# A two-block hybrid transformer on one core: first norm's weight row spread by TensorE, token sums in two steps, head halves joined by engines

## The chip, the cores and the metric

The kernel runs on one core of one Trainium2 chip. The metric is the device time of one execution in microseconds; the median of three runs stands for a kernel. One execution is also recorded by the hardware profiler, and all rows below are from that one. PE is TensorE's matmul side and PEld its weight loads, DVE is VectorE, ACT is ScalarE, POOL is GpSimd, SP is the engine that issues the DMAs.

## The reference, cut to what matters

All is float32: 512 tokens, 16 meta tokens ahead of them, width 1024.

```
def _rmsnorm(x, g): return x * rsqrt(mean(x*x) + EPS) * g

first block (once):
  h    = _rmsnorm([meta, x], norm_pre)                 # one weight row of 1024
  fox  = 8 causal heads of 64, decay bias; times silu(gate)
  mla  = 8 chunk-masked heads of 64 from low-rank q, kv; times silu(gate)
  x    = x + _rmsnorm([fox, mla] @ w_out, norm_post)

second block (two layers):
  h    = rms_norm(x, norm1)
  y_a .. y_d = mlstm, gqa (8 heads of 64), neighbourhood (8 heads of 64), differential attention
  x    = x + (sum_b sigmoid(gl_b) * (y_b @ w_up_b)) @ w_out
  h2   = rms_norm(x, norm2)
  x    = x + (silu(h2 @ w_gate) * (h2 @ w_up)) @ w_down     # d_ff = 2816 = 22 tiles of 128
out = rms_norm(x, final_g)
```

## The kernel before, in words

**Products.** A float32 operand is held as two float32r parts, `hi` and `lo`, and each product is three matmuls, hi·hi, lo·hi and hi·lo (`mm3`, L250 to L252). A weight tile is loaded as `raw`, rounded to `whi` by ACT (L221), and the rest `wlo` is taken by POOL or, every second or each time, by DVE (L223, `k.lo`). Results of PE stand in one of eight PSUM banks (`A`).

**Order.** PE runs in the order in which the program is written. For the other engines and the DMA issues a planner makes the order of each queue ahead of time, from estimated costs and from when the slots of the tile rings come free; on the chip each queue then runs strictly in its order. A tile tag is a ring of so many slots: `t2` six, `yn` three, `qs` two, `cb` two, `p` four.

**The start** (`first_block`, L681). SP loads token tile 0 in two halves, then the weight row `norm_pre`, spread by DMA over 128 partitions in two halves (`gain_row`, L528: tile `cb`), then token tiles 1 to 3 and the meta tokens. Each token tile is squared and summed by ACT (L720), scaled by DVE (L540), transposed by PE in eight pieces (L316) and split into `hi` and `lo` (L211, L212). The first weight product (`proj_late`, L268, matmuls L280) runs in two halves of 256 tokens; before the first half stand the transposes of tiles 0, 1 and 2, before the second that of tile 3 (`late_steps`, L152).

**Heads of 64** (`class Head`, L408; fox, mla, and branches b and c of both layers). The value tile of a head holds hi and lo side by side, so a head's output bank has two halves, partitions 0 to 63 and 64 to 127, that have to be added. After the last value matmul (L455) ACT copies the whole bank into a `t2` tile `z` (L458). When both heads of a pair are done, `pair_out` (L460) sends the upper half of one and the lower half of the other to the other partitions by two DMAs (L464, L465), and two DVE adds (L466, L467) make the joined tile `e`, which is gated or split. There are 24 pairs.

**The feed-forward** (`ffn`). Its 22 tiles of `d_ff` go in 11 pairs. The first pair runs as plain products: two gate tiles (each followed by `silu2`, L365 and L366, into `t2`), then two up tiles. Later pairs run as `fast_pair` (L582), a Strassen-Winograd scheme with seven products instead of eight; it needs sums of quarters of the tokens' activations, made once per layer by `Tokens.sums` (L563): two halves, each four DVE sums (L571 to L574) and for four results one ACT rounding (L576) and one DVE rest (L577). The quarters stand in two `qs` and two `cst` tiles. Those two `qs` slots also take the weights of the second member of each fast pair (`other` in `w_cols`), so the first such load waits until the sums have read a `qs` tile. In `fast_pair` the sums of weight blocks are L599 to L602, their rounding L591, the rest L592.

Of the kernel before, what the change touches and what calls it, by code (L numbers as in the profile page):

```python
# [18 lines left out]
P = 128  # L19
# [146 lines left out]
def hybrid_kernel(ctx: ExitStack, tc: tile.TileContext, i: dict, out: bass.AP):  # L166
# [241 lines left out]
    class Head:  # L408

        def __init__(self, v, blocks, meta=None):
            self.v, self.blocks, self.meta, self.pt, self.pm = v, blocks, meta, {}, {}

        def trans(self, t, p, col):

# [20 lines left out]
        def pv(self, t):  # L438

            if t % 2 == 0:  # L440
                return
            if t == 1:
                self.ps = bank()
            first, second = self.blocks(t - 1), self.blocks(t)
            ph, pl = self.pt[t // 2]
            parts = [(self.meta[0], *self.pm[t // 2], 0, 256)] if self.meta else []
            for b in sorted(set(first) | set(second), key=lambda b: not (b in first and b in second)):
                lo, hi = (0 if b in first else P), (256 if b in second else P)
                parts.append((self.v(b), ph[:, b], pl[:, b], lo, hi))
            o = (t // 2) * 256  # L450
            for j, (v, ph, pl, lo, hi) in enumerate(parts):
                last = j == len(parts) - 1
                passes = [(v, ph, P), (v[:, 0:64], pl, 64)]
                for w, q, m in (passes[::-1] if last else passes):
                    T_.matmul(self.ps[0:m, o + lo:o + hi], w, q[:, lo:hi], start=(j == 0 and m == P), stop=(last and m == P))  # L455
            if t == 3:
                self.z = t2()
                A_.copy(self.z, self.ps)  # L458

    def pair_out(heads):  # L460

        a, b = (h.z for h in heads)
        e = t2()
        nc.sync.dma_start(e[0:64], a[64:128])  # L464
        nc.sync.dma_start(e[64:128], b[0:64])  # L465
        V.tensor_tensor(e[0:64], a[0:64], e[0:64], ALU.add)  # L466
        V.tensor_tensor(e[64:128], b[64:128], e[64:128], ALU.add)  # L467
        return e

    def split_y(y, hi, lo):  # L470
        A_.copy(hi, y)
# [85 lines left out]
    class Tokens:  # L557
# [5 lines left out]
        def sums(self):  # L563

            (b11, b12), (b21, b22) = self.q
            hi = new(pool, [P, 4, 4, 256], "v", F32R, 1)
            lo = [new(pool, [P, 2, 4, 256], "ks", F32R) for _ in range(2)]
            self.t = [(hi[:, j], lo[j // 2][:, j % 2]) for j in range(4)]
            for c in (slice(0, 2), slice(2, 4)):
                t = [t2().rearrange("p (k c) -> p k c", k=2) for _ in range(4)]  # L570
                V.tensor_tensor(t[0], b12[:, c], b11[:, c], ALU.subtract)  # L571
                V.tensor_tensor(t[1], b22[:, c], t[0], ALU.subtract)
                V.tensor_tensor(t[2], b22[:, c], b12[:, c], ALU.subtract)
                V.tensor_tensor(t[3], b21[:, c], t[1], ALU.subtract)  # L574
                for j in (1, 2, 0, 3):
                    A_.copy(self.t[j][0][:, c], t[j])  # L576
                    V.tensor_tensor(self.t[j][1][:, c], t[j], f(self.t[j][0][:, c]), ALU.subtract)  # L577

        def quarter(self, a, b):
            return tuple(z[:, 4 * a:4 * a + 4, 256 * b:256 * b + 256] for z in self.h)  # L580
# [100 lines left out]
def first_block(k):  # L681
    nc, i, new, pool, A_, V, bank = k.nc, k.i, k.new, k.pool, k.A_, k.V, k.bank
    with k.tc.tile_pool(name="fb", bufs=1) as fb:
        k.fb = fb
        x, xm = new(pool, [P, NT, D], "x", bufs=1), new(pool, [NMETA, D], "v", bufs=1)
        for half in range(2):
            nc.sync.dma_start(x[:, 0, half * 512:half * 512 + 512], i["x"][0:P, half * 512:half * 512 + 512])
        gain = k.gain_row(i["norm_pre"], "cb")
        for t in range(1, NT):
            nc.sync.dma_start(x[:, t], i["x"][t * P:(t + 1) * P])  # L690
        nc.sync.dma_start(xm, i["meta"])
        cols = k.load(fb, i["cols_first"], "colsf")

        def col(name, n=P):
            a, w = COLS_FIRST[name]
            return cols[0:n, a:a + w]

        ss, hl = new(k.small, [P, 8], "xss"), k.act()
        h = k.tokens(hl)
        sm, xms = new(k.small, [P, 1], "mss")[0:NMETA], new(pool, [NMETA, D], "ks")  # L700

        def meta():
            A_.activation(xms, xm, AF.Square, accum_out=sm)
            r = k.rstd(sm, D, 1, NMETA)
            for half in range(2):
                sl = slice(half * 512, half * 512 + 512)
                V.scalar_tensor_tensor(xms[:, sl], xm[:, sl], r, gain[half][0:NMETA], ALU.mult, ALU.mult)

            def second():
                ps = bank()[:, 0:KD * NMETA]  # L710
                for kk in range(KD):
                    k.transpose(ps[:, kk * NMETA:(kk + 1) * NMETA], xms[:, kk * P:(kk + 1) * P], NMETA)
                k.evict_split(ps.rearrange("p (k c) -> p k c", k=KD), *(a[:, :, 0:NMETA] for a in hl))

            return second

        pending = []
        for t in range(NT):
            for half in range(2):
                A_.activation(k.t2(), x[:, t, half * 512:half * 512 + 512], AF.Square, accum_out=ss[:, 2 * t + half:2 * t + half + 1])  # L720
            pending.append(k.norm_tile(x[:, t], t, ss, h, gain))
        pending.append(meta())
        k.late = late_steps(pending[:-1]) + pending[-1:]
        k.constants()
        return first_body(k, fb, col, hl)


def first_body(k, fb, col, hl):
# [276 lines left out]
    def fox_head(hd):  # L1005
        u, e = fox.units[hd // 2], hd % 2
        st = Work()
        hobj = head(hd, *fox.v)
        fox.heads[hd] = hobj

        def sc(t):
            if t == 0:
                st.cb = new(pool, [P, L], "cb")
                nc.sync.dma_start(st.cb, fox.rows[hd].partition_broadcast(P))
            sps, n = scores(t, [(u.qs[:, e, t * P:(t + 1) * P], u.ks[:, 2 * e + b]) for b in range(2)], k.mcr)
            p = k.p_tile(n)

            r = k.softmax_of_sum([(sp, st.cb[:, a:b], a, b) for sp, a, b in sps], p)[1]
            V.tensor_scalar(p, p, r, None, ALU.mult)
            if t == 3 and hd in (1, 3):  # L1020
                v = fox.units[hd // 2 + 2]
                v.task = stream.push(fox_unit(v), U_COST, soon=True)
            return p

        def done():
            e = k.pair_out([fox.heads[hd - 1], fox.heads[hd]])
            V.scalar_tensor_tensor(e, e, 0.5, u.gate, ALU.mult, ALU.mult)
            y1[hd // 2] = k.y_tile()
            k.split_y(e, *y1[hd // 2])

        return [maps_of(hd, t, sc, hobj, done if t == 3 and hd % 2 else None, u) for t in range(NT)]
# [15 lines left out]
    def mla_head(hd):  # L1047
        u = mla.units[hd]
        hobj = head(hd, *mla.v)
        mla.heads[hd] = hobj  # L1050

        def sc(t):
            sl = slice(t * P, (t + 1) * P)
            (qh, ql), (kh, kl) = u.q, u.k
            sps, n = scores(t, [(qh[:, sl], kh), (qh[:, sl], kl), (ql[:, sl], kh)], k.mkr)
            p = k.p_tile(n)
            r = k.softmax_banks(sps, p)
            if t % 2:
                A_.activation(p, p, AF.Copy, bias=0.0, scale=r)
            else:  # L1060
                V.tensor_scalar(p, p, r, None, ALU.mult)
            if t == 3 and hd < 6:

                v = mla.units[hd + 2]
                v.task = stream.push(mla_unit(hd + 2, v), 1100)
                if hd % 2 == 0:
                    gate(hd // 2 + 1)
            return p

        def done():  # L1070
            j = hd // 2
            e = k.pair_out([mla.heads[hd - 1], mla.heads[hd]])
            V.scalar_tensor_tensor(e, e, 0.5, gates[j], ALU.mult, ALU.mult)
            if j >= 2:
                q = k.q_stack()
                y2.append((q[:, 0, 0:S], q[:, 1, 0:S]))
            k.split_y(e, *y2[j])

        return [maps_of(hd, t, sc, hobj, done if t == 3 and hd % 2 else None, u, q1) for t in range(NT)]
# [68 lines left out]
def ffn(k, x, l, h, quarters, last):  # L1148
# [30 lines left out]
    def pair(first):  # L1179

        if first:

            k.lo = 2
            gts, us = [k.silu2(plain(gw), k.t2()) for _ in range(2)], []
            tok.sums()
            for _ in range(2):
                us.append(plain(uw))
            k.lo = 1
# [352 lines left out]
def pair_maps(k, j, head, score, out, unit=None, before=None):  # L1541

    heads = [head(2 * j + e) for e in range(2)]

    def one(e, t):
        st = Work()
# [2 lines left out]
            st.p, st.col = score(e, t)  # L1549

        def done():
            out(k.pair_out(heads))

        needs = []
        if unit and e == 0 and t == 0:
# [444 lines left out]
```

## Time and profile before

| | us |
|---|---|
| three runs | 2560.34, 2564.12, 2567.02; median 2564.12 |
| the profiled execution | 2570.03 |
| its span, first to last instruction | 2568.2 |
| PE busy in the span | 2488.4 (97%) |
| DVE, ACT, POOL busy | 1602.7, 1329.6, 939.0 |
| TensorE's mean granted clock | 0.990 |

The profiled execution is 5.9 us above the median of the runs, and 1.8 us of it lie outside the span. A row of the waits reads "who waits, for whom: us in all, times, longest". A row of the timeline has start, length, engine, line, operation and tiles, and in brackets how long the engine had been idle and what released it. [...]

### The profile page before, as it was taken

What the parts mean: (1) busy time and instruction counts of PE and PEld (TensorE: products, weight loads), DVE (VectorE), ACT (ScalarE), POOL (GpSimd) and SP (SyncE); (2) the same over time, 40 slices, a digit from 0 to 9 for tenths busy, and PEclk for the clock granted to TensorE, in tenths of its full rate; (3) what the DMA queues carried; (4) which work ended last, traced back from release to release, by engine and by line L of the source; (5) the groups of instructions that cost most, each with busy time, mean ns of one, the idle gap of its engine ahead of it and who ended that gap; (6) DMA issues with size and microseconds to landing.
All of it is one profiled execution on the core that took longest, in us unless ns stands there. A gap on an engine that the chain in (4) does not pass through costs nothing. (4 is left out here: it accounts for less than half of the span.)

```text
span 2568.2 us, 39912 instructions
## 1 busy us (share of the span) xinstructions
PE 2488.4 (97%) x14358; PEld 2159.6 (84%) x14358; DVE 1602.7 (62%) x3521; ACT 1329.6 (52%) x2893; POOL 939.0 (37%) x834
## 2 busy tenths in 40 slices
PE   7999999999999999989999999999999999899998
PEld 7988788888888878779999888888878878799997
DVE  3577557769335354577888567584354464787886
ACT  4567646647445444354444467475354453554443
POOL 4453346542565544400000456424655534100002
PEclk9999999999999999999999999999999999999999
DMA  5552233221537332422333232214374334232232
GB/s 149 145 142 68 88 128 103 77 95 55 145 105 189 106 105 83 148 91 99 101 106 107 99 110 88 88 57 132 108 186 115 97 89 135 87 107 99 101 105 82
DMA packets 117750, 277.20 MB, mean 108 GB/s; under 512 B 15824, under 2 KB 37584, under 8 KB 117552
## 3 DMA queue, kind: packets, MB, share of 16 engines
q1 hardware_dynamic: 117552, 274.65, 35.4%
q8 instruction: 113, 1.85, 0.3%
q14 instruction: 85, 0.70, 0.1%
HBM read 230.26 MB, written 6.46 MB: 92 GB/s over the span
## 5 line engine op out<-in xcount | busy, mean ns | idle before, releaser
L223 POOL TENSOR_TENSOR wlo<-raw,whi 128x512 fp32r<-128x512 f32 (+4 forms) x481 | 617.4, 1286 | 622.9 <-ACT whi L221 598.8
L221 ACT CAST whi<-raw 128x512 fp32r<-128x512 f32 (+4 forms) x573 | 345.7, 605 | 513.5 <-PE A L251 331.8
L250 PE MATMUL A<-hi,whi 128*128 128x512 f32 (+2 forms) x1368 | 535.5, 391 | 0.7 <-ACT hi L211 0.7
L252 PE MATMUL A<-hi,wlo 128*128 128x512 f32 (+2 forms) x1368 | 515.5, 377 | 2.7 <-POOL wlo L223 2.7
L251 PE MATMUL A<-lo,whi 128*128 128x512 f32 (+2 forms) x1368 | 516.8, 378 | 0.1
L252 PEld LDWEIGHTS A<-hi,wlo 128*128 128x128 f32 x1368 | 258.4, 189 | 53.8 <-POOL wlo L223 3.5
L250 PEld LDWEIGHTS A<-hi,whi 128*128 128x128 f32 x1368 | 258.7, 189 | 37.9 <-ACT hi L211 0.8
L251 PEld LDWEIGHTS A<-lo,whi 128*128 128x128 f32 x1368 | 259.1, 189 | 37.1 <-DVE lo L212 0.3
L651 POOL TENSOR_TENSOR ptl<-raw,pth 128x512 fp32r<-128x512 f32 x20 | 26.0, 1320 | 605.7 <-ACT pth L650 605.7
L212 DVE TENSOR_TENSOR ptl<-A,pth 128x512 fp32r<-128x512 f32 (+3 forms) x256 | 148.9, 582 | 103.9 <-ACT pth L211 102.5
L316 PE MATMUL A<-ident,p 128*128 128x128 f32 (+3 forms) x1125 | 176.2, 279 | 22.9 <-DVE p L540 17.5
L250 PE MATMUL A<-v,whi 128*128 128x256 f32 x640 | 182.3, 285 | 10.7 <-ACT whi L591 10.7
L316 PEld LDWEIGHTS A<-ident,p 128*128 128x128 f32 (+3 forms) x1125 | 136.5, 140 | 62.1 <-DVE p L540 19.7
L252 PE MATMUL A<-v,wlo 128*128 128x256 f32 x640 | 181.9, 284 | 3.8 <-DVE wlo L592 3.8
L251 PE MATMUL A<-ks,whi 128*128 128x256 f32 x640 | 181.2, 283 | 0.0
L344 ACT ACTIVATE p<-p,sms 128x512 f32<-128x512 f32 (+6 forms) x160 | 100.6, 629 | 121.0 <-DVE sms L342 116.1
L211 ACT CAST pth<-A 128x512 fp32r<-128x512 f32 (+3 forms) x256 | 128.0, 500 | 65.8 <-PE A L316 64.3
L223 DVE TENSOR_TENSOR wlo<-raw,whi 128x512 fp32r<-128x512 f32 x92 | 67.0, 728 | 125.4 <-ACT whi L221 125.2
L298 PE MATMUL A<-whi,hi 128*128 128x256 f32 (+7 forms) x440 | 144.5, 328 | 0.0
L300 PE MATMUL A<-whi,lo 128*128 128x256 f32 (+7 forms) x440 | 141.7, 322 | 0.0
L299 PE MATMUL A<-wlo,hi 128*128 128x256 f32 (+7 forms) x440 | 141.6, 322 | 0.0
L250 PEld LDWEIGHTS A<-v,whi 128*128 128x128 f32 x640 | 122.4, 191 | 17.2 <-ACT whi L591 11.2
(433 smaller groups left out, 6172.7 us busy)
## 6 DMA issues: line engine op xcount, KB each, us to landing
raw<-in_t_gl_dram SPq DMA_DIRECT2D x64, 512.0 KB, 3.5
raw<-in_w_ffn_down_dram SPq DMA_DIRECT2D x44, 512.0 KB, 3.6
raw<-in_w_in_dram SPq DMA_DIRECT2D x26, 512.0 KB, 3.5
raw<-in_w_out_dram SPq DMA_DIRECT2D x24, 512.0 KB, 3.6
raw<-in_t_gate_dram SPq DMA_DIRECT2D x24, 512.0 KB, 3.6
raw<-in_t_up_dram SPq DMA_DIRECT2D x24, 512.0 KB, 3.5
qs<-in_t_gate_dram SPq DMA_DIRECT2D x20, 512.0 KB, 4.4
qs<-in_t_up_dram SPq DMA_DIRECT2D x20, 512.0 KB, 4.2
```

What stands on the lines that cost most here:

```text
L211: A_.copy(hi, ps)
L212: V.tensor_tensor(lo, ps, f(hi), ALU.subtract)
L221: A_.copy(hi, src)
L223: (V if k.lo and k.turn % k.lo == 0 else G).tensor_tensor(lo, src, f(hi), ALU.subtract)
L250: T_.matmul(ps, sh, mh, start=first, stop=False, **kw)
L251: T_.matmul(ps, sh, ml, start=False, stop=False, **kw)
L252: T_.matmul(ps, sl, mh, start=False, stop=last, **kw)
L298: T_.matmul(ps, sh, wh[:, j], start=(b + j == 0), stop=False)
L299: T_.matmul(ps, sh, wl[:, j], start=False, stop=False)
L300: T_.matmul(ps, sl, wh[:, j], start=False, stop=(b + j == nk - 1))
L316: T_.transpose(dst, src, ident[0:k, 0:k])
L344: A_.activation(dst, dst, AF.Exp, bias=st[:, e:e + 1], scale=-1.0, accum_out=st[:, 2:3])
```

## The change

Four edits:

1. **First norm's weights.** The two halves of `norm_pre` are loaded as rows of one partition (2 KB each) into slices of two `yn` tiles. Each is split into hi and lo on one partition, multiplied by a row of ones with two matmuls of one contraction row each, and the bank is copied to the `cb` tile, the first half by DVE and the second by ACT. The spreading DMAs are gone.
2. **Order of the first product.** Tiles 0 and 1 are transposed, then comes the first half of the tokens, then tiles 2 and 3, the second half, the meta tokens.
3. **Feed-forward.** `sums` yields after each half: the first half is issued after the first gate tile and the second after the second gate tile. The two gates are kept in `yn` instead of `t2`.
4. **Joins.** A pair has one tile `e`. When a head's last value matmul is done, ACT copies the half that has to change partitions from PSUM to the pair's tile (64x512), and DVE adds the other half from PSUM onto it. The copy to `z`, the two DMAs and `pair_out` are gone.

```
             if t == 3:
-                self.z = t2()
-                A_.copy(self.z, self.ps)
-
-    def pair_out(heads):
-        a, b = (h.z for h in heads)
-        e = t2()
-        nc.sync.dma_start(e[0:64], a[64:128])
-        nc.sync.dma_start(e[64:128], b[0:64])
-        V.tensor_tensor(e[0:64], a[0:64], e[0:64], ALU.add)
-        V.tensor_tensor(e[64:128], b[64:128], e[64:128], ALU.add)
-        return e
+                self.e = self.mate.e if self.mate else t2()
+                own, other = (slice(64, P), slice(0, 64)) if self.mate else (slice(0, 64), slice(64, P))
+                A_.copy(self.e[own], self.ps[other])
+                V.tensor_tensor(self.e[own], self.ps[own], self.e[own], ALU.add)
...
         def sums(self):
...
                 for j in (1, 2, 0, 3):
                     A_.copy(self.t[j][0][:, c], t[j])
                     V.tensor_tensor(self.t[j][1][:, c], t[j], f(self.t[j][0][:, c]), ALU.subtract)
+                yield
...
-        gain = k.gain_row(i["norm_pre"], "cb")
+        raw = [k.gate_tile()[0:1] for _ in range(2)]
+        for half in range(2):
+            nc.sync.dma_start(raw[half], i["norm_pre"][half * 512:half * 512 + 512].unsqueeze(0))
         for t in range(1, NT):
             nc.sync.dma_start(x[:, t], i["x"][t * P:(t + 1) * P])
         nc.sync.dma_start(xm, i["meta"])
+        ones = new(fb, [1, P], "ones", F32R)
+        k.G.memset(k.f(ones), 1.0)
+        gain = [new(pool, [P, L], "cb")[:, 0:512] for _ in range(2)]
+        for half in range(2):
+            (hi, lo), ps = (k.t2(F32R)[0:1] for _ in range(2)), bank()
+            (A_.copy if half else V.tensor_copy)(hi, raw[half])
+            V.tensor_tensor(lo, raw[half], k.f(hi), ALU.subtract)
+            k.T_.matmul(ps, ones, hi, start=True, stop=False)
+            k.T_.matmul(ps, ones, lo, start=False, stop=True)
+            (A_.copy if half else V.tensor_copy)(gain[half], ps)
...
-        k.late = late_steps(pending[:-1]) + pending[-1:]
+        k.late = pending[0:2] + [(0, S // 2)] + pending[2:4] + [(S // 2, S)] + pending[4:]
...
         if first:
             k.lo = 2
-            gts, us = [k.silu2(plain(gw), k.t2()) for _ in range(2)], []
-            tok.sums()
+            gts, us, sums = [], [], tok.sums()
+            for _ in range(2):
+                gts.append(k.silu2(plain(gw), k.gate_tile()))
+                next(sums)
```

The callers of `pair_out` (fox, mla, `pair_maps`) set `mate` of the second head to the first and take its `e`.

## Rows read from the trace of the kernel before

**Rows 1.** The page, part 1: busy time of each engine over the whole span.
```profile
PE 2488.4 (97%) x14358; PEld 2159.6 (84%) x14358; DVE 1602.7 (62%) x3521; ACT 1329.6 (52%) x2893; POOL 939.0 (37%) x834
```

**Rows 2.** The waits over the whole span: us in total, times, longest.
```profile
PE A L250 <- ACT whi L591: 10.7, 2, 5.5
PE A L455 <- DVE ptl L212: 6.8, 4, 2.4
PE A L252 <- DVE wlo L592: 3.8, 2, 2.0
PE A L815 <- DVE v L212: 2.3, 1, 2.3
PE A L1776 <- issue: 1.8, 1, 1.8
DVE t L466 <- DMA t<-t: 32.9, 13, 6.1
```

**Rows 3.** Busy time by stretch, around layer 0's first fast pair.
```profile
1104.00:1125.00 21.00, 21.00 (x109) 17.69 (x108) 14.55 (x21) 11.08 (x19) 4.35 (x3) 1.00 0.36 109
1125.00:1137.00 12.00, 4.71 (x24) 4.35 (x24) 11.93 (x21) 4.96 (x10) 0.00 (x0) 0.72 0.29 87
1137.00:1146.00 9.00, 9.00 (x78) 9.00 (x77) 7.15 (x13) 5.85 (x11) 0.00 (x0) 1.00 0.36 117
```

**Rows 4.** The timeline there: DVE, SP and ACT, in order of time.
```profile
1120.71 0.68 DVE L571 TENSOR_TENSOR t<-qs,qs 128x512 f32<-128x512 f32 x1
...
1121.47 0.33 SPq L242 DMA_DIRECT2D qs<-in_t_gate_dram  x1
...
1126.13 0.68 DVE L599 TENSOR_TENSOR p<-qs 128x512 f32<-128x512 f32 x1
...
1129.64 1.66 ACT L591 CAST whi<-p 128x512 fp32r<-128x512 f32 x3 [1.91 <-DVE p L600]
```

**Rows 5.** Busy time by stretch at the start; last column GB/s of the DMAs.
```profile
4.00:7.00 3.00, 0.00 (x0) 0.00 (x0) 0.82 (x3) 0.72 (x2) 0.55 (x1) 1.00 0.77 179
7.00:10.00 3.00, 1.31 (x5) 0.91 (x6) 1.00 (x2) 0.00 (x0) 0.00 (x0) 1.00 1.01 386
```

**Rows 6.** The timeline of the start, all engines.
```profile
1.64 0.90 SPq L532 DMA_DIRECT2D cb<-in_norm_pre_dram  x2
...
6.49 0.75 DVE L540 SCALAR_TENSOR_TENSOR p<-x,rstd,cb 128x512 f32<-128x512 f32 x1 [1.26 <-DMA cb<-in_norm_pre_dram]
...
9.00 0.75 DVE L540 SCALAR_TENSOR_TENSOR p<-x,rstd,cb 128x512 f32<-128x512 f32 x1 [1.76 <-DMA cb<-in_norm_pre_dram]
...
10.49 0.63 ACT L720 ACTIVATE t<-x 128x512 f32<-128x512 f32 x1 [5.64 <-DMA x<-in_x_dram]
...
18.16 0.56 PE L280 MATMUL A<-hi,whi 128*128 128x256 f32 x1
```

**Rows 7.** DMA issues in the first 20 us: KB each, us to landing.
```profile
x<-in_x_dram SPq DMA_DIRECT2D x2, 256.0 KB, 2.4
```

**Rows 8.** Lines by source: duration in ns, shortest, median, longest.
```profile
L466 DVE TENSOR_TENSOR t<-t,t x24: 672/682/1794, 119.1 to 1949.8; 64x512 f32<-64x512 f32 x24
L458 ACT COPY t<-A x48: 558/585/589, 96.1 to 1948.8; 128x512 f32<-128x512 f32 x48
L509 DVE TENSOR_TENSOR x<-x,A x112: 673/678/689, 1080.3 to 2561.2; 128x512 f32<-128x512 f32 x112
```

**Rows 9.** Busy time by stretch, around joins; 190 to 200 holds no disturbance.
```profile
178.00:188.00 10.00, 7.41 (x33) 5.60 (x33) 7.54 (x24) 5.08 (x15) 3.63 (x3) 0.66 0.20 54
190.00:200.00 10.00, 10.00 (x57) 8.39 (x56) 7.43 (x26) 8.01 (x25) 5.12 (x6) 1.00 0.29 92
209.00:219.00 10.00, 6.32 (x28) 5.88 (x28) 7.74 (x18) 3.61 (x11) 2.27 (x2) 0.66 0.06 23
1925.00:1931.00 6.00, 3.63 (x14) 2.95 (x14) 4.63 (x10) 3.06 (x8) 2.97 (x4) 0.74 0.41 122
```

**Rows 10.** The timeline of DVE at the join of the third fox pair.
```profile
179.31 1.03 DVE L466 TENSOR_TENSOR t<-t,t 64x512 f32<-64x512 f32 x1 [0.96 <-DMA t<-t]
```

More of the change, by code (lines that the diff above doesn't have):

```diff
@@ L413, in __init__ @@
         def __init__(self, v, blocks, meta=None):
-            self.v, self.blocks, self.meta, self.pt, self.pm = v, blocks, meta, {}, {}
+            self.v, self.blocks, self.meta, self.pt, self.pm, self.mate = v, blocks, meta, {}, {}, None
         def trans(self, t, p, col):
@@ L1009, in fox_head @@
         fox.heads[hd] = hobj
+        hobj.mate = fox.heads[hd - 1] if e else None
         def sc(t):
@@ L1025, in done @@
         def done():
-            e = k.pair_out([fox.heads[hd - 1], fox.heads[hd]])
+            e = hobj.e
             V.scalar_tensor_tensor(e, e, 0.5, u.gate, ALU.mult, ALU.mult)
@@ L1050, in mla_head @@
         mla.heads[hd] = hobj
+        hobj.mate = mla.heads[hd - 1] if hd % 2 else None
         def sc(t):
@@ L1071, in done @@
             j = hd // 2
-            e = k.pair_out([mla.heads[hd - 1], mla.heads[hd]])
+            e = hobj.e
             V.scalar_tensor_tensor(e, e, 0.5, gates[j], ALU.mult, ALU.mult)
@@ L1543, in pair_maps @@
     heads = [head(2 * j + e) for e in range(2)]
+    heads[1].mate = heads[0]
     def one(e, t):
@@ L1551, in done @@
         def done():
-            out(k.pair_out(heads))
+            out(heads[1].e)
         needs = []
```

## The prediction

> **What bounds the kernel now.** I read the busy times first: PE is busy for 2488 of 2568 us, VectorE for 62%, the others less [rows 1]. So an edit pays only where it takes away time in which PE stands still or runs below its full clock. The second view is the list of waits, for PE alone: 80 us of idle time fall into many small waits, and the question is which of them the four edits touch [rows 2]. The third view, busy time by stretch, gives what a wait really costs, as it also shows the slower clock after it: I count matmuls per us in a disturbed stretch against a quiet one beside it. The timeline then says which instruction PE was waiting for. The change adds four matmuls and takes none away, so PE's own work stays, and the forecast is a sum of stalls.
>
> **Feed-forward sums: the largest term.** The first fast pair of a layer waits for ACT's rounding at L591 and then for DVE's rest at L592, in both layers, 10.7 and 3.8 us together [rows 2]. In layer 0 the stretch from 1125 to 1137 holds 24 matmuls in 12 us, the one behind it 78 in 9 us, that is 8.7 per us; 24 need 2.8 us, so 9.2 us are lost, and the granted clock, 0.72 on average there, is in that figure [rows 3]. The cause stands in the timeline: DVE's first sum of the second half is at 1120.71 and frees a `qs` slot; SP issues the second gate weight into it at 1121.47; DVE can add it at 1126.13; ACT rounds the sum of weights at 1129.64, and PE starts [rows 4]. PE had been ready since 1125, so the chain is 5 to 8 us too late, from the sums.
>
> Why were they late? DVE had room: in the 21 us before 1125 it was busy for 14.55, so 6.45 us were idle [rows 3]. The two sum halves were one block after the second `silu2`, and needed `t2` tiles, of which the two gates and their tanh tiles held four of six. After the change the first half is issued behind the first gate and the gates no longer hold `t2`. The work itself is the same 16 DVE instructions of a layer. How much comes back has two bounds. Upper: all 9.2 us of a layer. Lower: VectorE may become the bound itself. Between 1104 and 1137 it did 14.55 + 11.93 = 26.5 us of work [rows 3]; with PE 9.2 us ahead the same point lies at 1127.8, and 23.8 us are left for it. If every one of these instructions were needed by then, 2.7 us of the wait would stay, and 6.5 come back. Some are not needed then (the rests for later products, the next pair's split), so I take 8 of 9.2 per layer: **16 us** for two layers, bounds 12 and 18.4. The bound drops further if the sums stand ahead of a `wlo` that PE needs for the plain products; that is a rival below. The weight behind the `qs` slot comes earlier by as much as the sums do; the DMAs' share was 0.36 in that stretch, so there is room for it [rows 3].
>
> **Joins.** Removed per pair: two DMAs with their SP issues. Kept: two ACT copies and two DVE adds. ACT copies 64 instead of 128 partitions of the same 512 columns, 0.585 us today, and I take the same. The DVE add now has one operand in PSUM; the nearest row is the residual add L509, 0.678 us (never over 0.689 in 112), against 0.682 for today's SBUF add, which rose to 1.79 us at times [rows 8]. So the engines' work is level. [...]
>
> What goes away is DVE standing in its queue for a join's DMA: 32.9 us in 13 times, the longest 6.1 [rows 2]. Behind it in the same queue stand the rests `ptl` that PE's value matmuls need, and softmax steps; the third fox pair is the plain case, where L466 comes after 0.96 us of idling and takes 1.03 us [rows 10]. What PE lost there, against 57 matmuls in 10 us in the quiet stretch, 5.7 per us [rows 9]:
> - third fox pair, 178 to 188: 33 matmuls need 5.8 us, 4.2 lost, at a mean clock of 0.66;
> - last fox pair, 209 to 219: 28 need 4.9, 5.1 lost. PE waits there for value rests behind the join in DVE's queue, 2.3 us [rows 2], but the first scores of the next branch have a chain of their own, so I count half, 2.6;
> - third pair of branch c in layer 1, 1925 to 1931: 14 need 2.5, 3.5 lost;
> - the wait of L1776, 1.8 us [rows 2]: its keys go through DVE and SP behind a join that was late;
> - of the 6.8 us of L455 waiting for `ptl`, two of the four are in the stretches above and make about 4.6; of the rest, 2.2, I count half, 1.1.
>
> Together 13.2. Against it: each of 48 adds now waits in DVE's queue for an ACT copy of 0.58 us [rows 8], and what is queued behind it waits too. The trace of before has no such wait at this place. Bounds: nothing, where DVE would idle or the planner puts other work between, and 48 x 0.58 = 28 us of DVE time. DVE is idle for 38% [rows 1] and PE feels only what it is waiting for at that moment; with the 13 long waits of before costing PE 13.2 us at 32.9 us of waiting, 0.4 us of PE per us of wait, and an add that arrives just behind its copy in perhaps one case in ten, I put 1.2 us. Joins: **12 us**, bounds 4 (only the waits named, half of them taken over by the next) and 18.
>
> **Start.** The spread weight row is 512 KB of writes: while it goes, from 4 to 7 us, the DMAs move 179 GB/s, after it 386 [rows 5]. The 0.54 MB of these 3 us would need 1.4 at the higher rate. So token tile 1, which ACT waits 5.64 us for and gets at 10.49 [rows 6], can come some 1.6 us earlier by the rate, and up to 3 by the bytes; I take 2. The row itself: issued where the spread was, at 1.64 [rows 6], and landing like the token halves after 2.4 us [rows 7], at about 4.5. Then a one-partition copy and a rest, priced by their 512 columns as L458 and L509 [rows 8], two matmuls of 0.5 us each as L280 [rows 6], and a copy out of 0.6: 4.5 + 0.6 + 0.7 + 1.0 + 0.6 = 7.4 for the first half and a little later for the second, against 6.49 and 9.00 now [rows 6]. The first is later by 0.9, the second earlier by 1, and both are ahead of tile 1. The new order lets the first weight matmuls, now at 18.16, start without tile 2's eight transposes; these run later on PE all the same, so only idle time is won, 0.5. **2.5 us**; bounds -1 (the chain late, tile 1 held by something else) and 4.
>
> **Sum.** 16 + 12 + 2.5 = 30.5 us. Against the profiled execution of 2570.0 this gives 2539.5. That execution is 5.9 us above the median of the runs, 2564.1, whose forecast is therefore 2533.6; I say 2534.
>
> **Rivals.**
> (a) *VectorE takes over as the bound of the first pair.* The eight instructions of a half, 8 x 0.68 = 5.4 us, stand ahead of a `wlo` that PE's plain tiles need, or the idle 6.45 us is not filled. For it: DVE is busy 11.93 of 12 us from 1125 [rows 3]. Against it: that is the backlog, and before it a third of the time is free. The sums give 3 instead of 8 per layer: 2564.1 - 20.5 = 2543.6.
> (b) *The next wait inherits the joins.* In branch c the bias loads and in mla the softmax chain are close behind; the clock stays low as PE still pauses. Joins give 4: 2541.6. With (a) together 2551.6.
> (c) *Slower: PSUM banks are held longer.* Today a head's bank is free after ACT's copy; afterwards the DVE add has to have run too, 0.68 us plus its turn in the queue, for 48 heads [rows 8]. If PE needs that bank at once, 1.0 us per head costs 48 us against 30.5 won: 2582. It decides from about 0.8 us a head ((30.5 + 7.7) / 48). Against it: there are eight banks, and no wait of PE in the list names the copy L458.
> (d) *It does not do what it says.* The planner orders the queues anew for other ring slots, new blockings of some 25 us in all appear elsewhere and eat the gain: 2559.
>
> **How the numbers follow.** Forecast as summed 0.60; (a) 0.15; (b) 0.10; both 0.05; (d) 0.06; (c) 0.04. Faster by over 0.3%, 7.7 us and about what a measurement of this kernel can tell from no change, are the first four: 0.90; within it 0.06; slower 0.04. The sum's own bounds are -1 + 12 + 4 = 15 and 4 + 18.4 + 18 = 40.4, that is 2549 and 2524; to reach (a) with (b), and some stalls beyond those counted, the range is 2521 to 2553.
>
> **What would show it.** In the profile of the changed kernel: the waits L250 for L591 and L252 for L592 gone or under 2 us each, and the stretch around a layer's first fast pair at a granted clock of 1.00; L571's second half some 6 us earlier against the gates than now. No wait of DVE for a DMA of a join, and PE's waits of L455 for `ptl` down from 6.8 to about 3. The first L280 at about 15.5 instead of 18.16. The prediction is wrong if PE waits for `wlo` in the plain tiles, if a wait on a head's add releases PE's banks, or if waits appear in places that the edits do not touch.

## The result and the profile after

| | before | after |
|---|---|---|
| median of the runs, us | 2564.77 (four, 2560.34 to 2567.02) | 2533.78 (four, 2532.69 to 2537.01) |
| the profiled execution, us | 2570.03 | 2537.01 |
| its span, us | 2568.2 | 2534.7 |
| TensorE's mean granted clock | 0.990 | 0.997 |

The ratio is 0.988, with an interval of 0.987 to 0.990: the changed kernel is 31.0 us faster by the medians, against a forecast of 30.5. The two profiled executions differ by 33.0; the table of matmuls below says which 2 us or so of that belong to these two executions and not to the change. The parts of the sum came out less exact than their total.

The changed kernel's lines are shifted. The token sums are now L565 to L571, the first fast pair's weight sums L594 to L597 with their rounding L586 and rest L587. A head's copy and add are L461 and L462, the value matmuls L456. The weight row is L695 to L699, the squares L728, the scaling L534.

**The page**, part 1, of the changed kernel:

```profile
PE 2476.6 (98%) x14362; PEld 2148.8 (85%) x14362; DVE 1601.0 (63%) x3525; ACT 1335.8 (53%) x2895; POOL 935.9 (37%) x835
```

PE has four matmuls more and is busy for 11.8 us less than in [rows 1]: fewer of the same matmuls ran at the lower clock (the mean granted clock is 0.997 against 0.990). The rest of the 33.5 us of span is idle time that is gone.

**The waits of PE** in the changed kernel, us in total, times, longest:

```profile
PE A L316 <- DVE p L534: 6.5, 5, 4.0
PE A L697 <- DVE t L695: 4.5, 1, 4.5
...
PE A L280 <- ACT hi L211: 2.3, 2, 1.9
...
PE A L252 <- DVE wlo L587: 2.1, 2, 1.1
...
PE A L250 <- DVE t L618: 1.4, 2, 0.7
...
PE A L823 <- DVE sms L342: 1.1, 1, 1.1
...
PE A L823 <- DMA cb<-frows: 0.9, 1, 0.9
...
PE A L456 <- DVE yl L212: 0.6, 1, 0.6
```

Against [rows 2]: the wait for the rounding of the first fast pair, 10.7 us, is gone, and 2.1 of 3.8 remain of the wait for its rest. The value matmuls' 6.8 us of waiting for `ptl` are gone. Two small waits of L823 are new; they stand at 152 and 182 us, in fox's scores behind the second and the third join, and the part on the rivals comes back to them. The rows for L534, L697 and L280 are the start, where no PE work covers anything, before or after.

**The stretches** of the changed kernel that hold the same matmuls, to within two or three at the edges, as those of [rows 3] and [rows 9] (columns: busy us of PE, PEld, DVE, ACT and POOL, with the number of instructions in brackets, mean granted clock of TensorE as a share of the full one, DMA share, GB/s), the third fox pair, the last fox pair, the first fast pair of layer 0, and the third pair of branch c:

```profile
176.60:183.50 6.90, 5.09 (x35) 3.58 (x34) 6.83 (x19) 5.20 (x15) 3.72 (x3) 1.00 0.22 59
204.50:208.70 4.20, 3.98 (x31) 3.84 (x29) 3.95 (x11) 2.94 (x10) 1.44 (x3) 1.00 0.13 55
1108.50:1113.00 4.50, 3.43 (x26) 3.03 (x26) 4.50 (x9) 2.72 (x6) 0.00 (x0) 1.00 0.39 116
1901.40:1903.50 2.10, 2.10 (x14) 1.81 (x14) 1.88 (x4) 0.72 (x3) 2.10 (x2) 1.00 0.28 94
```

What took 10, 10, 12 and 6 us takes 6.9, 4.2, 4.5 and 2.1, and the granted clock is 1.00 in all four. The first and third rows also show what bounds them now: DVE is busy for 6.83 of 6.90 us and for all of 4.50.

**The timeline** of the changed kernel around the feed-forward's first pair, DVE, SP and ACT (start, length):

```profile
1087.55 0.69 DVE L565 TENSOR_TENSOR t<-qs,qs 128x512 f32<-128x512 f32 x1
...
1093.16 1.78 DVE L568 TENSOR_TENSOR t<-cst,t 128x512 f32<-128x512 f32 x1
...
1096.07 0.68 DVE L565 TENSOR_TENSOR t<-qs,qs 128x512 f32<-128x512 f32 x1
...
1096.82 0.33 SPq L242 DMA_DIRECT2D qs<-in_t_gate_dram  x1
...
1103.05 0.68 DVE L594 TENSOR_TENSOR p<-qs 128x512 f32<-128x512 f32 x1
...
1106.85 1.67 ACT L586 CAST whi<-p 128x512 fp32r<-128x512 f32 x3 [0.65 <-DVE p L595]
```

The chain is that of [rows 4], link by link. The second half's first sum is at 1096.07 instead of 1120.71, 24.6 us earlier in the trace and about 8 us earlier against PE's work, which is itself 16.2 us ahead here. The load follows 0.75 us behind it as before, and the first rounding is ready at about 1107.5, 1 us ahead of the pair's first matmul at 1108.6.

**The joins.** Where DVE waited 32.9 us in 13 places for a join's DMA [rows 2], it now waits for ACT:

```profile
DVE t L462 <- ACT t L461: 33.7, 24, 4.7
```

And the view of that one line, L462, of the changed kernel (who waited for it, at the end):

```profile
L462 DVE TENSOR_TENSOR t<-A,t x48: 659/688/696, 94.5 to 1921.8; 64x512 f32<-64x512 f32 x48
...
who waited for it (us, times):
  ACT yh L465: 2.4, 4
  ACT yh L1798: 2.2, 4
  PEld A L823: 1.1, 1
  POOL cb L1786: 1.0, 1
```

So DVE stands as long as before, and PE hardly feels it: its one entry here is a weight load of L823, 1.1 us. An add that reads PSUM takes 688 ns against 682 of the old one in SBUF [rows 8]: 6 ns more, or 0.3 us in 48 adds.

### The profile page after: what moved, and what is told of

It reads as the page before. It is cut to its first block, busy times and chain, and to the rows that moved or that the text cites. A ratio compares the mean times of both kernels' runs of the same rounds, so it can differ in the third digit from the quotient of the medians.

```text
span 2534.7 us, 39821 instructions
## 1 busy us (share of the span) xinstructions
PE 2476.6 (98%) x14362; PEld 2148.8 (85%) x14362; DVE 1601.0 (63%) x3525; ACT 1335.8 (53%) x2895; POOL 935.9 (37%) x835
## 5 line engine op out<-in xcount | busy, mean ns | idle before, releaser
L586 ACT CAST whi<-p 128x512 fp32r<-128x512 f32 x160 | 98.9, 621 | 63.4 <-PE A L251 57.5
```

## Where the time came from, matmul by matmul

All kernels here issue the same 14,358 matmuls in the same order (the start edit puts four in front and swaps some transposes before the first 43 us). So each matmul of one trace can be paired with its counterpart in another, and where the difference of their start times grows, time was won. The table has the steps over 0.9 us of the whole change, in stretches of 10 us of the kernel before, and beside them those of three kernels that have one edit each (the next section). A dash is less than 0.9 us; steps that only kernels with one edit show are left out.

| place, us in before | whole change | joins alone | sums alone | start alone |
|---|---|---|---|---|
| up to 43 | +2.4 | +1.2 | +2.0 | +2.7 |
| 143 to 153, fox's scores behind the second join | -1.0 | -1.0 | - | - |
| 173 to 183, third fox pair | +3.2 | +3.3 | - | - |
| 203 to 223, last fox pair | +5.9 | +6.0 | - | - |
| 273 to 293, mla | +1.7 | +1.7 | - | - |
| 573 to 583, layer 0, maps | +1.7 | +1.5 | +1.5 | - |
| 813 to 823, value matmul waiting for `ptl` | +1.7 | +1.6 | - | - |
| 1123 to 1133, feed-forward 0 | +6.7 | - | +6.7 | - |
| 1423 to 1433 | -1.0 | -1.1 | -1.0 | -1.0 |
| 1883 to 1893 | +1.6 | +1.6 | +1.6 | +1.6 |
| 1923 to 1933, branch c, third pair | +4.2 | +3.9 | - | - |
| 2233 to 2243, feed-forward 1 | +7.2 | - | +7.2 | - |

Steps that one edit alone shows, and the whole change too, belong to that edit: joins 3.2 + 5.9 + 1.7 + 1.7 + 4.2 - 1.0 = 15.7 us, sums 6.7 + 7.2 = 13.9. Some 2 us of the 15.7 may be that one execution of before: against the trace of sums alone, the same places of the changed kernel give 13.9. Steps that stand in columns of edits which have nothing in common don't belong to an edit: +1.7 at 573, +1.6 at 1883 and -1.0 at 1423 are what the one profiled execution of before had and others did not. Together, 2.3 us, they are most of why the profiled pair differs by 2.0 us more than the medians. The first line belongs there in part: the unchanged start of the second and third kernels is itself 1.2 and 2.0 us ahead of that execution.

## The experiments

Each ratio is against the kernel before on the same chip; whole-change runs gave 0.9883 and 0.9885.

### One edit at a time

Theory: the three terms add up and each sits in its own place. Rival: an edit alone finds the next wait behind it, or the edits only work together. The three edits are those of the diff ahead; each kernel has one of them and is otherwise the kernel before.

```
joins_alone:  only Head (e, own, other), the callers' mate, pair_out gone
sums_alone:   only yield in sums, gates in gate_tile(), next(sums) behind each gate
start_alone:  only gain row by matmul, and k.late's new order
```

> The kernel before with the join edit alone. Lined up matmul by matmul, the changed kernel's trace gains about 17 us in the stages of heads of 64 (start of the second block's branches left out). Theory: these gains belong to the joins, since VectorE's queue no longer stands for a DMA; then 2565 - 17 = 2548 us, and the same four places gain (third and fourth fox pair, branch c of both layers). Rival: part of it came from the queues being planned anew after the other edits; then 2555 or more, and other places gain.

> The kernel before with the feed-forward edit alone. Theory: 6.7 and 7.2 us in the two layers' first fast pair, as in the changed kernel's trace, whatever else is changed: 2565 - 14 = 2551 us. Rival: the gain needs the t2 slots that the join edit sets free as well; then 2558 or more.

> The kernel before with the weight row by TensorE and the new order of the first product alone. Theory: 2.4 us at the first matmul of the second product (L250, 264 columns), 29.3 to about 27.0 us, and nothing later: about 2562 us, which the timing can hardly tell from no change. Rival: the start is absorbed by later waits for weights; then the end stands where it stood, although the first products are earlier.

| | median, us | ratio to before |
|---|---|---|
| joins alone | 2554.72 | 0.9952 (0.9937 to 0.9966): 12.3 us won |
| sums alone | 2554.42 | 0.9947 (0.9932 to 0.9962): 13.6 us won |
| start alone | 2571.05 | 1.0013 (0.9997 to 1.0029): 3.3 us lost, or nothing |

The sums are worth the 14 us that were expected of them. The joins are worth less than the 17 expected of this run, 12.3 with an interval of 8.6 to 16.2, though at the expected places. The table shows that the two don't touch each other's places. The start edit shows no gain by itself (its interval allows 0.8 us), although its trace is 2.7 us ahead at the first weight products: it loses 2.0 us at 183 to 193, 1.5 at 773 to 783 and 1.0 each at 1133 and 1423, and ends where before's ends.

The three add up to 22.6 us against 30 for the whole. Each has an interval of about 4 us to either side, which covers the gap; whether the edits also help one another was not settled by this.

### The whole change again, and without the start

To see the start edit where it is used, the changed kernel was timed with and without it on one chip. The second kernel has the spread load `gain_row` and the old order of the first product back.

```
-        raw = [k.gate_tile()[0:1] for _ in range(2)]
...
+        gain = k.gain_row(i["norm_pre"], "cb")
...
-        k.late = pending[0:2] + [(0, S // 2)] + pending[2:4] + [(S // 2, S)] + pending[4:]
+        k.late = late_steps(pending[:-1]) + pending[-1:]
```

> The changed kernel once more, unaltered, as the neighbour of the next one on the same chip: a ratio of 0.988 to the kernel before, some 31 us less.

> The changed kernel without its start: weight row spread by DMA and the old order of the first product, joins and sums as in the changed kernel. Theory: the start edit is worth what the traces show at the first matmuls, 1.5 us (mean of three traces each way) to 2.4: this one is slower than the changed kernel by 1 to 3 us. Rival, after the start edit alone gave a ratio of 1.0013: it only plans the queues anew and this one is as fast or faster by up to 4 us.

Unaltered it took 2536.78 us (2535.92 to 2540.84), ratio 0.9885 (0.9868 to 0.9903). Without the start edits it took 2533.94 (2532.89 to 2539.21), ratio 0.9873 (0.9855 to 0.9891). So the third term of the sum does not show in the time; if anything the kernel is better without. In these two traces the kernel with the edit is 1.2 us ahead at 30 us and 3.4 behind at the end. Most of the difference collects at two places: 1.8 us at about 760 us, a spot that also differs between executions of one kernel (last section), and 1.2 us at 2050, where the granted clock fell to 0.50 with the edit and not without.

### What the joins' gain is made of

The edit takes away two transfers and two issues a pair, and with them DVE's wait for a landing. Theory: the wait alone made the cost, since the `ptl` rests and softmax steps stand behind it in DVE's queue. Rival: the transfers or SP's issues themselves cost. So the transfers were put back as loads that nobody reads: 48 DMAs between partition halves, 64x384 each. In the first form they read the joined tile `e`, which the gate then overwrites.

```
                 V.tensor_tensor(self.e[own], self.ps[own], self.e[own], ALU.add)
+                nc.sync.dma_start(spare[other], self.e[own][:, 0:384])
```

> The changed kernel, and after each of the 48 joining adds SP also sends 64 rows of 384 columns of the joined tile to a spare tile that nobody reads (96 KB where the kernel before sent 128 KB). The output does not change. Theory: what the joins cost was VectorE standing for the DMA in its queue, not the transfer or its issue; the time stays at 2534, within 3 us. Rival: the issues on SP (48 of about 0.5 us) and the traffic were the cost; then at least 8 us come back, 2542 or more.

It took 2542.26 us, ratio 0.9902 (0.9887 to 0.9916), some 5 us more than the change and the time that the rival had named. But this form brings a wait of its own: the in-place gating has to let the read finish first. The waits of this kernel:

```profile
DVE t L1039 <- DMA spare<-t: 3.6, 3, 2.5
...
DVE t L1086 <- DMA spare<-t: 2.4, 1, 2.4
```

So it didn't separate the two. The second form reads the finished, split output `y`, which nothing overwrites soon; and a third issues the same 48 DMAs with one row each instead of 64.

```
+    def traffic(y):
+        for a, b in ((slice(0, 64), slice(64, 128)), (slice(64, 128), slice(0, 64))):
+            nc.sync.dma_start(spare[a], f(y[b, 0:384]))
...
             k.split_y(e, *y1[hd // 2])
+            k.traffic(y1[hd // 2][0])
```

> The earlier kernel with kept join traffic read the joined tile, and the gating of that tile had to wait for the read: part of its loss may be that wait. Here the two transfers of a pair (64 rows of 384 columns each, 48 in all, to a spare tile nobody reads) read the finished y tile, which nothing overwrites soon. Output unchanged. Theory: a transfer that no engine waits for costs nothing; ratio to the kernel before about 0.988 as the changed kernel, within 3 us. Rival: the transfers and their issues on SP delay weights and stacks, 5 us or more come back (2541 and up).

> As the one before, but each of the 48 transfers moves one row of 384 columns instead of 64: SP's issues stay, the bytes go. If the one before loses time and this one does too, it is the issues in SP's queue; if only the one before does, the bytes; theory: neither, ratio about 0.988.

Full transfers: 2538.10 us, ratio 0.9875 (0.9861 to 0.9890). One row each: 2538.86, ratio 0.9880 (0.9865 to 0.9895). Both are the ratio of the change without them, so the time shows no cost of transfers and issues; an interval of about 4 us to either side could hide one.

Paired matmul by matmul with before, the traces say more. In both kernels the gains at the fox pairs and in mla stay whole, 3.2, 5.9 and 1.8 us: there transfers and issues were free, which leaves the waiting of DVE's queue for a landing as what the edit removed. The third pair of branch c is another matter. Its step is 3.9 to 4.2 us in all eight traces with the join edit and without such transfers, and 0.0 with the full ones and 2.6 with one row each. The timeline of DVE there, first before, then the changed kernel:

```profile
1924.23 0.42 DVE L342 CUSTOM_DVE_ANT_0 p<-A,cb 128x256 f32<-128x256 f32 x1 [4.86 <-POOL cb L1773]
...
1925.38 1.56 DVE L466 TENSOR_TENSOR t<-t,t 64x512 f32<-64x512 f32 x1 [0.72 <-DMA t<-t]
```

```profile
1899.98 0.42 DVE L342 CUSTOM_DVE_ANT_0 p<-A,cb 128x256 f32<-128x256 f32 x1 [2.59 <-POOL cb L1786]
...
1900.33 0.55 DVE L212 TENSOR_TENSOR ptl<-A,pth 128x384 fp32r<-128x384 f32 x1
```

With the full transfers, the same step of DVE and then two waits over the whole span:

```profile
1903.35 0.42 DVE L342 CUSTOM_DVE_ANT_0 p<-A,cb 128x256 f32<-128x256 f32 x1 [4.60 <-POOL cb L1795]
```

```profile
POOL cb L1795 <- DMA cb<-in_c_rpb_z_dram: 66.3, 32, 5.4
PE A L462 <- DVE ptl L212: 2.4, 1, 2.4
```

In before DVE stood here 4.86 us for a bias that GpSimd adds, and then 0.72 for the join's landing; the add took 1.56, and PE's `ptl` came behind it. In the change the `ptl` follows the bias step at once. With the transfers back no add stands in between, but DVE stands 4.60 us for the bias instead of 2.59, the bias step comes 3.2 us later against PE's work, and PE waits 2.4 us for `ptl` again. GpSimd waits 66.3 us for these bias loads with the full transfers and 68.6 with one row each, against 53.4 in the change and 63.3 in before; the first form, which has the transfers too, shows 53.8. So at this place the gain also needs the transfers and issues to be gone, and the wait for a landing is not shown as its whole cause. These are one trace each; how often the stall comes is not known.

### Why the sums were late: ring slots or their place in the program

The prediction gave the slots of `t2` as the reason: four of six were held by gates and tanh. The diff changes two things together, the gates' ring and the step at which the sums are issued. Two kernels undo one each.

```
sums_gates_t2:
-                gts.append(k.silu2(plain(gw), k.gate_tile()))
+                gts.append(k.silu2(plain(gw), k.t2()))
sums_one_step:
             for _ in range(2):
                 gts.append(k.silu2(plain(gw), k.gate_tile()))
+            for _ in range(2):
                 next(sums)
```

> The changed kernel with the two gates back in t2, sums still in two steps. Theory: the sums were late for want of t2 slots; then with four of six slots held the second half waits again, and PE waits 3 us or more per layer at the first fast pair (1.2 and 0.9 in the changed kernel). Rival: the place in the program was what counted; then PE's waits there stay at about 2 us per layer.

> The changed kernel with the gates in yn, but both steps of the sums issued behind the second gate as before. Theory (slots): with the slots free the planner hoists the sums into VectorE's idle time anyway, and PE waits about 2 us per layer as in the changed kernel. Rival (place in the program): the sums stand behind the second silu2 again and PE waits 5 us or more per layer.

With the gates back in `t2` it took 2536.02 us, and PE's matmuls around the first pair are 1.3 and 1.5 us later in the two layers. With both halves behind the second gate it took 2548.07, and they are 6.8 and 6.7 us later. (One timed execution each; the two layers agree, and the second kernel's 11.3 us over the change on that chip compare with a range of 4.9 us in the change's own runs.) The waits of PE in the second kernel:

```profile
PE A L250 <- ACT whi L586: 8.8, 2, 4.4
...
PE A L252 <- DVE wlo L587: 5.1, 4, 2.3
```

And its timeline of DVE:

```profile
1091.66 0.68 DVE L565 TENSOR_TENSOR t<-qs,qs 128x512 f32<-128x512 f32 x1
...
1095.73 1.23 DVE L593 TENSOR_TENSOR ptl<-raw,pth 128x1024 fp32r<-128x1024 f32 x1 [3.39 <-ACT pth L592]
...
1102.73 0.68 DVE L565 TENSOR_TENSOR t<-qs,qs 128x512 f32<-128x512 f32 x1
1103.49 0.33 SPq L242 DMA_DIRECT2D qs<-in_t_gate_dram  x1
```

The first sum runs at 1091.66, and then DVE stands for 3.39 us in its fixed queue at L593, waiting for an ACT rounding, with 15 instructions of the sums behind it. The second half comes at 1102.73, 6.7 us later than in the change, and so does the load. This kernel is the one before in all of this stretch but for the gates' ring: freeing the slots alone won next to nothing (13.9 us of these two waits, 14.5 in [rows 2]). The place in the program sets the time, and once the place is right the slots are worth another 1.4 us a layer.

### What is left in the first pair: DVE, and a way out that failed

DVE is busy without a gap there, so six of the eight rests of a layer's sums were given to GpSimd, which is busy for 1.65 of the 31 us from 1095 to 1126. Theory: PE's last 2.1 us of waiting for L587 go. Rival: GpSimd's work takes DVE's time.

```
-                    V.tensor_tensor(self.t[j][1][:, c], t[j], f(self.t[j][0][:, c]), ALU.subtract)
+                    (G if c.start == 0 or j in (0, 3) else V).tensor_tensor(self.t[j][1][:, c], t[j], f(self.t[j][0][:, c]), ALU.subtract)
```

> The changed kernel with six of the eight rests of the token sums of a layer (L571) on GpSimd, which is idle from 1102 to 1126 us. Theory: VectorE, busy 12.00 of 12 us at the first fast pair, is what still holds PE there (about 2.1 us per layer); 6 x 0.6 = 3.6 us of VectorE's work less takes these waits away: 2 to 4 us faster than the changed kernel. Rival: GpSimd's rests at 1.3 us each come too late for the products, or its weight rests behind them, and PE waits longer.

It took 2545.13 us, ratio 0.9902 (0.9885 to 0.9918), 5 us worse than the change; in the one trace the two first pairs lose 4.2 and 4.5 us. Its timeline of DVE and POOL, and then its longest wait of PE:

```profile
1095.00 3.11 POOL L571 TENSOR_TENSOR ks<-t,v 128x512 fp32r<-128x512 f32 x2 [0.30 <-ACT v L570]
1095.17 1.78 DVE L567 TENSOR_TENSOR t<-cst,qs 128x512 f32<-128x512 f32 x1
...
1099.76 3.44 POOL L571 TENSOR_TENSOR ks<-t,v 128x512 fp32r<-128x512 f32 x2
1100.28 1.77 DVE L565 TENSOR_TENSOR t<-qs,qs 128x512 f32<-128x512 f32 x1
```

```profile
PE A L252 <- DVE wlo L223: 7.2, 2, 3.6
```

A DVE sum that runs beside a rest on GpSimd (median 1.74 us) takes 1.77 or 1.78 us instead of 0.68. A rest moved off DVE saves 0.68 us there and gives 1.1 back to every sum that runs beside it. The backlog now reaches a `wlo` that plain tiles need: rival (a) of the prediction, produced on purpose. The wait for L587 did fall, to 0.7 us.

### The start: does ACT's wait for the row set it?

In the changed kernel's start the second half row lands late and holds ACT's queue:

```profile
1.65 0.58 SPq L685 DMA_DIRECT2D yn<-in_norm_pre_dram  x2
...
3.96 0.41 DVE L695 CAST t<-yn 1x512 fp32r<-1x512 f32 x1 [0.62 <-DMA yn<-in_norm_pre_dram]
...
6.02 0.62 ACT L695 CAST t<-yn 1x512 fp32r<-1x512 f32 x1 [4.01 <-DMA yn<-in_norm_pre_dram]
6.54 0.62 ACT L728 ACTIVATE t<-x 128x512 f32<-128x512 f32 x1
...
8.93 0.75 DVE L534 SCALAR_TENSOR_TENSOR p<-x,rstd,cb 128x512 f32<-128x512 f32 x1 [0.68 <-POOL rstd L312]
9.00 0.56 ACT L699 COPY cb<-A 128x512 f32<-128x512 f32 x1
...
15.83 0.58 PE L280 MATMUL A<-hi,whi 128*128 128x256 f32 x1 [1.91 <-ACT hi L211]
```

Token tile 0 is there at about 3.3 us (the kernel below squares it then), and its squares stand behind the rounding of a row until 6.54. So the row was loaded by one 4 KB DMA, and both halves rounded by DVE.

```
+        raw_row = k.raw_tile()[0:1]
+        raw = [raw_row[:, 0:512], raw_row[:, 512:1024]]
+        nc.sync.dma_start(raw_row, i["norm_pre"][0:D].unsqueeze(0))
...
-            (A_.copy if half else V.tensor_copy)(hi, raw[half])
+            V.tensor_copy(hi, raw[half])
```

> The changed kernel with the weight row loaded by one DMA of 4 KB and both halves rounded by VectorE. In the changed kernel ACT stands until 6.02 us for the second half of the row and squares tile 0 only from 6.54 (3.19 before). Theory: ACT's wait moves tile 0's chain; without it the squares start at about 3.2 and the first weight product 1 us earlier than 15.83. Rival: tile 1's data sets the start, and it stays at 15.8.

It took 2538.68 us in one timed execution. Its timeline:

```profile
3.30 0.63 ACT L728 ACTIVATE t<-x 128x512 f32<-128x512 f32 x1 [1.29 <-DMA x<-in_x_dram]
...
8.11 0.75 DVE L534 SCALAR_TENSOR_TENSOR p<-x,rstd,cb 128x512 f32<-128x512 f32 x1 [0.68 <-POOL rstd L312]
...
10.51 0.56 ACT L699 COPY cb<-A 128x512 f32<-128x512 f32 x1
...
16.38 0.58 PE L280 MATMUL A<-hi,whi 128*128 128x256 f32 x1 [1.64 <-ACT hi L211]
```

The squares come 3.2 us earlier, the first scaling 0.8, and the first weight matmul 0.55 us later: the copy of the second gain half now stands behind the squares in ACT's queue, at 10.51 instead of 9.00. The expected 1 us did not come. The wait that was taken away was real, and another step of the same queue took its place; it shows nothing on what an order without either would give.

## Why the prediction was right, and where it was right for another reason

**Total.** 2534 was forecast, 2533.8 measured. That is closer than its terms deserve: by the trace, feed-forward and start were put too high and joins too low; by the runs of one edit each, joins were right.

**Feed-forward sums: 16 forecast, 13.9 in the trace, 13.6 alone.** The place, the chain and its order were right. Two things were off. The size, 8 of 9.2 us per layer, is 6.7 and 7.2: DVE is busy without a gap in the stretch from 1108.5, as the working behind 6.5 assumed, and the waits for L587 and L618 keep 2.1 and 1.4 us. The instructions that I took for not yet needed lifted the gain above 6.5 by 0.2 and 0.7 only; twice 6.5 is 13, so by its own working the lower bound was 13 and not 12. And the reason was wrong: not the held `t2` slots but the place at which the sums are issued set their time. The diff does both, so the forecast didn't suffer; for a change that had only moved the gates the same working would have promised 16 us and missed them all.

**Joins: 12 forecast, 15.7 in the trace, 12.3 alone.** The gain stands at the forecast places. The mechanism is shown for the fox pairs and mla, where putting back transfers and issues costs nothing. For the third pair of branch c it is shown in part only: there DVE had stood mostly for a late bias and 0.72 us for the join, and with the transfers back the gain is gone. Term by term: third fox pair 4.2 forecast, 3.2 measured; last fox pair 5.1 lost of which half counted, 5.9 measured, so the halving was the mis-sized step: the next branch's scores had no delay of their own to show; branch c 3.5 forecast, 4.2 measured; mla 1.7, not forecast; value matmuls elsewhere 1.1 forecast, 1.7 measured. For the 1.8 us of L1776 no step of its own over 0.9 us shows. The cost of the new wait was put at 1.2 us; the one loss that only the join edit shows is 1.0, at 153 us.

How that 1.2 was reached does not hold, though. It rested on 0.4 us of PE per us of DVE waiting. The new adds wait 33.7 us, as long as the old ones, and no step of the table shows PE losing by it: the loss of 1.0 is a wait of PE for an add itself, rival (c). That 1.2 and 1.0 agree is luck. The number of waits is 24 instead of 13, the mean 1.4 instead of 2.5 us; that short waits end before PE runs dry is a reading of these rows, and no run here tested it.

**Start: 2.5 forecast, nothing in the time.** The trace of the pair shows the forecast 2.4 us at the first products, the first L280 at 15.83 against a forecast of 15.5, and the higher rate of the loads: from 4 to 7 us they move 275 GB/s instead of 179 [rows 5]; from 7 to 10 us it is 288 instead of 386, so over the six us the totals are equal. But the step from "PE begins earlier" to "the kernel ends earlier" failed. The lead at the first products is real: one and the same matmul lies at 41.5 to 43.5 us in four traces with the old start and at 40.4 to 41.3 in nine with the new one (leaving out the row loaded by one DMA, 42.8), 1.5 us earlier in the mean. It does not reach the end, and the runs with and without the edit can't be told apart; what takes it back is not known. The forecast's own working was also off in a link: the second row half was used at 6.02 us, not at about 4.5, and held ACT.

**Rivals.** (a), DVE as the bound of the first pair, is half true: DVE is the bound, but of 2 us a layer, not 6. (b) came only in small: behind the third fox pair PE now waits 1.1 us for a softmax step (L823 for L342), about what that pair is short of its forecast. (c), a wait that the prediction had named as a sign of being wrong, came once. The 1.0 us lost at 153 is a scores matmul that starts at 151.98 in the changed kernel; its weight load waits 1.1 us for a join's add, which ends at 151.93, while the row of PE for the same moment names a DMA. In before the matmul starts at 153.29, right behind ACT's copy, which ends at 153.24. The kernel with the full transfers names the add for PE too:

```profile
PE A L829 <- DVE t L468: 0.9, 1, 0.9
```

By the program a PSUM bank is all that the scores and the add share; the trace does not name banks. It is one head of 48, so (c) cost 1.0 us and not 48. (d) is out.

**A hit by chance in part.** The chain from the profiled execution to the median was a subtraction of 5.9 us. The table shows that the execution held some 2.3 us (1.7 + 1.6 - 1.0) that belong to no edit; another execution would have had other stalls to count. By the trace, the sum's errors are +2.1 for the sums, +2.5 for the start and -3.7 for the joins, and cancel to within a microsecond.

No version here beats the changed kernel beyond its interval; the one without the start edits equals it with less in it.

## What to carry to other kernels

Between engines with fixed queues, look at what stands *behind* a wait for a DMA: at the fox pairs and in mla here the transfers themselves were free, and an engine that waited for them in its queue cost PE some 11 us, while the same length of waiting on a neighbour engine cost about 1. But look also at the loads that run beside such transfers: in branch c one bias step came 3.2 us later with them, and a gain of 4.2 us was gone in that trace. When a block of small work feeds a later stage, issue it in pieces at the places where the engine has time; where a piece stands decided more here, 6.8 and 6.7 us in the two layers, than which buffers it holds, 1.3 and 1.5. Time won ahead of the first product is not won at the end until runs with and without it show it.

## What the runs showed of the hardware that was not expected

- **DVE beside GpSimd.** A DVE add of two SBUF tiles, 0.68 us alone, takes 1.77 us while a GpSimd subtraction of SBUF tiles (median 1.74 us) runs. The changed kernel holds such a pair by itself (L568, 1.78 us at 1093.16, in the timeline above, beside a GpSimd `wlo` of 1.66 us from 1092.74). So in these traces the DVE instruction is stretched to about the length of the other; why, they don't show.
- **Half clock that comes or not at the same place.** The same pause of PE, 2.19 and 2.07 us ahead of eight transposes in layer 0's maps, was followed by a stretch at a mean granted clock of 0.88 in the execution of before and of 1.00 in that of after; no edit touches this place. First before, then after:

```profile
570.00:584.00 14.00, 11.60 (x49) 9.10 (x48) 10.52 (x21) 6.80 (x16) 4.31 (x4) 0.88 0.20 71
```

```profile
558.00:572.00 14.00, 11.72 (x60) 9.20 (x59) 12.26 (x24) 8.57 (x20) 5.18 (x4) 1.00 0.21 70
```

  The granted clock fell to 0.50 ten times in before's execution, for 3.4 or 6.8 us each, and three times in after's, for 3.4 us (not counting the last 5 us of each); the table's lines at 573 and 1883 are two places where it did in one execution and not in another, and each moved the time by about 1.6 us. So one trace can price such a place by that much too high or too low.
- **A small load behind large ones.** The two 2 KB rows were issued together at 1.65 us, behind two loads of 256 KB from 0.73 us; the first was used at 3.96 and the second at 6.02, so a landing is not a constant of its size.
- **A spot that differs from run to run.** At 760 to 770 us of the changed kernel, where stacked loads land, the unaltered kernel's second trace is 1.6 us behind its first, and four variants that edit nothing near it 1.1 to 3.8 us behind. Differences of single traces there say nothing on an edit.
